# Seven half-depth products in place of eight: the last output projection of a two-layer trunk kernel, with its conditioning moved into layer 1

## The chip, the core and the metric

The kernel runs on one core of a Trainium2 chip. A core has a matrix engine (PE, with a weight-load side PEld), a vector engine (DVE), a scalar engine (ACT), a general engine (POOL) and a queue engine (SP). Each takes its instructions in order. PE writes only to PSUM, 8 banks of 512 fp32 per partition; all else lies in SBUF, 128 partitions wide. Loads are issued on SP's queue, most stores on POOL's. The metric is the device time of one execution in microseconds, as the median of several runs.

## The reference

Two transformer layers act on 640 tokens (512 latent, 128 context) of width 2048, in fp32. What is changed belongs to the end of layer 1:

```python
m = jax.nn.silu(cond) @ w + b            # modulation: shift, scale, gate of a layer
...
y_c = o_c...reshape(b, t, C_W) * jax.nn.silu(cg)
y_d = merge_heads(attend(q_d, dk_all, dv_all)) * jax.nn.silu(dg)
return jnp.concatenate([y_c, y_d], axis=-1) @ w_out, new
...
xp = xp + gt_p * out_p
xs = xs + gt_s * out_s
```

So the output projection of layer 1 is a product of a 2048 x 2048 weight with the 2048 x 640 transposed activations y, and each output row is scaled by a gate `gt` that comes from the conditioning and added to the residual.

## The kernel before

Activations are kept transposed: 128 channels on the partitions, 640 tokens along the row, so y is 16 tiles `y[k]` of 128x640. A projection is cut into output tiles of 128 channels. One tile sums over 16 channel blocks k, in four quarters of four. fp32 accuracy is had from two reduced-precision parts: `split` (L211) writes hi = ACT copy and lo = DVE subtraction, for weights (`wh`, `wl`, 128x512 for a quarter) and for activations (`h`). For each k, `proj_q` (L237) issues three matmuls (L244 to L246: wh·hi, wh·lo, wl·hi) on each half of the tokens, HV, 320 columns each, into PSUM `pa` and `pb`. A tile is thus 16 x 3 x 2 = 96 matmuls of 320 columns.

`run_tiles` (L277) runs a list of tiles. The first three ("leads") are computed together, quarter by quarter, while `make_h` brings in the activations; the third uses the PSUM of attention, `Sp`. After that tile follows tile. `run_ahead` (L322) keeps weight loads (`raw`) 5 and splits 3 quarters ahead, with 4 buffers each. After every quarter `slot` (L269) advances unfinished work: `prep` (what follows a finished tile), `attn` (attention of a head pair) and a filler at a given rate.

The filler is the conditioning, `ada_on_dve` (L171): for a block of 512 columns, 16 loads `adaw` and 32 DVE multiply-adds of 128x512 (L182, L184), then four matmuls with ones (L190) and two transposes (L196) on PE. The last three blocks (`fill2`) give the gate of layer 1 and run in the last projection (L1153), one step for each quarter.

In that last projection `y_maker` (L670) loads y back from DRAM (`yin<-yd`, L677), but for tiles 6, 7, 14 and 15, which are still in SBUF. `fin_job` (L1120) then loads the residual (`xr<-xd`), adds the gated tile to it (`fin_sum`, L1117, three DVE operations), transposes five blocks back to rows (L396), copies them (ACT, L1128 and L1129) and stores them from POOL's queue (L1130, L1131). The last tile is done in halves (`fin_last`, L1134) and stored from SP's and ACT's queues.

The order on each engine is made by a scheduler when the program is built: it may move instructions of an engine past each other where their data allow it.

## Time and profile before

| what | value |
|---|---|
| median of 3 runs | 2360.15 us (2356.45 to 2361.38) |
| the profiled execution, its own time | 2359.36 us |
| its span in the profile | 2357.6 us |
| granted clock of PE, mean | 0.996 |
| HBM read, written | 273.62 MB, 27.79 MB |
| DMA packets | 370061, 304.08 MB, mean 129 GB/s |
| first matmul of the last projection, from the span's start | 2115.3 us |

The profile is one execution. Busy time alone doesn't say what sets the end; the chain of waits (the work that ended last, followed back) and the tables by stretch do. A matmul's recorded time overlaps with that of the next one, since they are pipelined: the pace of PE is read from the distance of starts.

### The profile page before, as it was taken

What the parts mean: (1) busy time and instruction counts of PE and PEld (TensorE: products, weight loads), DVE (VectorE), ACT (ScalarE), POOL (GpSimd) and SP (SyncE); (2) the same over time, 40 slices, a digit from 0 to 9 for tenths busy, and PEclk for the clock granted to TensorE, in tenths of its full rate; (3) what the DMA queues carried; (4) which work ended last, traced back from release to release, by engine and by line L of the source; (5) the groups of instructions that cost most, each with busy time, mean ns of one, the idle gap of its engine ahead of it and who ended that gap; (6) DMA issues with size and microseconds to landing.
All of it is one profiled execution on the core that took longest, in us unless ns stands there. A gap on an engine that the chain in (4) does not pass through costs nothing.

```text
span 2357.6 us, 40891 instructions
## 1 busy us (share of the span) xinstructions
PE 2321.4 (98%) x16188; PEld 2244.9 (95%) x16188; DVE 1372.3 (58%) x2728; ACT 870.4 (37%) x1837; POOL 126.9 (5%) x173
## 2 busy tenths in 40 slices
PE   6999999999999999999999999999999999999999
PEld 3788999999999999999999999999999999999999
DVE  4458766756845565667955445354445554576662
ACT  4325442433422223222553444334334434453221
POOL 0001000000000000000010100001000000000000
PEclk8999999999999999999999999999999999999999
DMA  9984425425444445666431222212221212236552
GB/s 324 324 268 136 138 75 160 137 59 160 139 130 125 146 135 187 192 192 196 129 92 57 79 72 72 73 51 86 63 77 55 70 56 71 72 112 216 182 172 78
DMA packets 370061, 304.08 MB, mean 129 GB/s; under 512 B 16737, under 2 KB 310174, under 8 KB 369358
## 3 DMA queue, kind: packets, MB, share of 16 engines
q1 hardware_dynamic: 362464, 273.78, 38.2%
q0 software_dynamic: 6864, 27.47, 3.1%
q8 instruction: 127, 2.08, 0.3%
q14 instruction: 64, 0.52, 0.1%
q10 hardware_dynamic: 542, 0.22, 0.0%
HBM read 273.62 MB, written 27.79 MB: 128 GB/s over the span
## 4 chain that ended last, share of the span: by engine, by line
PE 93%; DMA 2%; DVE 2%; ACT 1%; issue 1%; SPq 0%; POOL 0%; ACTq 0%; DVEq 0%; POOLq 0%
PE pa L244 13%; PE pb L244 13%; PE pb L245 13%; PE pb L246 13%; PE pa L245 13%; PE pa L246 13%; PE T L545 2%; PE S L557 1%; PE S L559 1%; PE S L558 1%; PE T L158 1%; PE T L396 1%; PE T L606 1%; DMA ada<-in_ada_w 1%; PE T L608 1%
## 5 line engine op out<-in xcount | busy, mean ns | idle before, releaser
L212 ACT ACTIVATE wh<-raw 128x512 fp32r<-128x512 f32 (+1 forms) x550 | 344.0, 626 | 1044.9 <-PE pb L245 925.9
L213 DVE TENSOR_TENSOR wl<-raw,wh 128x512 fp32r<-128x512 f32 (+1 forms) x550 | 375.4, 683 | 552.5 <-ACT wh L212 501.1
L244 PE MATMUL pa<-h,wh 128*128 128x320 f32 x2112 | 669.9, 317 | 1.8 <-ACT h L747 1.2
L245 PE MATMUL pa<-h,wh 128*128 128x320 f32 x2112 | 655.8, 311 | 0.4 <-DVE h L213 0.4
L244 PE MATMUL pb<-h,wh 128*128 128x320 f32 x2112 | 654.3, 310 | 0.0
L246 PE MATMUL pa<-h,wl 128*128 128x320 f32 x2112 | 654.0, 310 | 0.0
L246 PE MATMUL pb<-h,wl 128*128 128x320 f32 x2112 | 653.9, 310 | 0.0
L245 PE MATMUL pb<-h,wh 128*128 128x320 f32 x2112 | 653.4, 309 | 0.0
L244 PEld LDWEIGHTS pa<-h,wh 128*128 128x128 f32 x2112 | 397.3, 188 | 22.0 <-issue 16.4
L245 PEld LDWEIGHTS pa<-h,wh 128*128 128x128 f32 x2112 | 398.4, 189 | 4.4 <-issue 3.3
L246 PEld LDWEIGHTS pb<-h,wl 128*128 128x128 f32 x2112 | 396.7, 188 | 2.5 <-issue 2.5
L246 PEld LDWEIGHTS pa<-h,wl 128*128 128x128 f32 x2112 | 397.3, 188 | 0.8 <-issue 0.8
L244 PEld LDWEIGHTS pb<-h,wh 128*128 128x128 f32 x2112 | 396.9, 188 | 0.5 <-ACT h L747 0.4
L245 PEld LDWEIGHTS pb<-h,wh 128*128 128x128 f32 x2112 | 396.9, 188 | 0.4 <-issue 0.4
L184 DVE SCALAR_TENSOR_TENSOR acc<-adaw,sT,acc 128x512 f32<-128x512 f32 x480 | 338.1, 744 | 18.4 <-DMA adaw<-in_ada_w 17.9
L531 ACT ACTIVATE p<-S,nm,rq 128x768 f32<-128x768 f32 (+3 forms) x120 | 101.2, 844 | 108.8 <-DVE nm L526 80.6
L524 DVE TENSOR_REDUCE nm<-S 128x1 f32<-128x768 f32 (+3 forms) x120 | 91.9, 766 | 23.3 <-PE S L559 22.6
L212 ACT ACTIVATE pth<-T 128x512 fp32r<-128x512 f32 (+1 forms) x132 | 65.8, 533 | 69.6 <-PE T L545 67.4
L213 DVE TENSOR_TENSOR ptl<-T,pth 128x512 fp32r<-128x512 f32 (+1 forms) x132 | 77.3, 608 | 5.2 <-ACT pth L212 3.9
L545 PE MATMUL T<-ident,p 128*128 128x128 f32 x452 | 64.5, 273 | 0.1
L465 ACT COPY qsw<-qx 32x512 f32<-32x512 f32 x96 | 59.3, 618 | 5.6 <-DVE m L441 4.2
L668 POOL DMA_DIRECT2D yd<-y x32 | 18.0, 562 | 750.4 <-DVE y L823 515.4
(251 smaller groups left out, 2295.2 us busy)
## 6 DMA issues: line engine op xcount, KB each, us to landing
adaw<-in_ada_w SPq DMA_DIRECT2D x256, 256.0 KB, 2.9
raw<-in_od_w_in SPq DMA_DIRECT2D x208, 256.0 KB, 2.8
raw<-in_ev_w_in SPq DMA_DIRECT2D x202, 256.0 KB, 3.0
ada<-in_ada_w SPq DMA_DIRECT2D x16, 2048.0 KB, 10.5
raw<-in_ev_w_out SPq DMA_DIRECT2D x64, 256.0 KB, 3.9
raw<-in_od_w_out SPq DMA_DIRECT2D x64, 256.0 KB, 2.7
yd<-y POOLq DMA_DIRECT2D x32, 320.0 KB, 2.9
yin<-yd SPq DMA_DIRECT2D x28, 320.0 KB, 4.6
```

The costliest lines, as they stand in the source:

```text
L158: PE.matmul(acc[32 * g:32 * g + 32, 0:wd], sT[:, kt, :], w[:, kt % m, :], start=(kt < 4), stop=(kt >= KT - 4), tile_position=(0, 32 * g))
L184: V.scalar_tensor_tensor(out=acc[c], in0=w, scalar=sT[:, kt, c:c + 1], in1=acc[c], op0=ALU.mult, op1=ALU.add)
L212: A.activation(hi, x, AF.Copy)
L213: V.tensor_sub(lo, x, hi)
L244: PE.matmul(ps, wh[:, i, :], hi[:, sl], start=(j == js[0] if alone else (pos == 0 and j == 0)), stop=False)
L245: PE.matmul(ps, wh[:, i, :], lo[:, sl], start=False, stop=False)
L246: PE.matmul(ps, wl[:, i, :], hi[:, sl], start=False, stop=(j == js[1] - 1 if alone else (pos == 3 and j == 3)))
L396: PE.transpose(t[:, i * P:(i + 1) * P], src(b), ident)
L465: A.copy(sw[32 * d:32 * d + 32, :], x[32 * (d ^ 1):32 * (d ^ 1) + 32, 0:NS])
L524: V.tensor_reduce(nm, s, axis=AX.X, op=ALU.max, negate=True)
L531: A.activation(p[:, 0:n], s, AF.Exp, scale=rsc, bias=nm, accum_out=l)
L545: PE.transpose(t[:, i * P:(i + 1) * P], p, ident)
```

## The change

Tiles 0 to 3 of the last projection are computed as before (0 to 2 as leads, 3 alone). Tiles 4 to 15 go in six pairs. A pair is a product of a 2x2 block matrix of weights (two tiles by two halves of the 16 k blocks: A11, A12, A21, A22) with a 2x2 block matrix of activations (two halves of k by two halves of the tokens: B11, B12, B21, B22). `run_pairs` does it with seven products in place of eight, Q1, Q2, N5, P6, P7, Q3, P4 in this order, each of 8 k blocks x 3 = 24 matmuls of 320 columns into a bank `pq`.

The weight sums (N5: A21+A22, P6: that plus A11, P7: A11+A21, Q3: that plus A12) are made by DVE on fp32 weights, in `sx` and `sf`, ahead of the split. The sums of activations T1 to T4 are the same for all pairs: `forms` makes them once, four DVE subtractions of 320 columns and a split of 960 for each of 8 k, from a second load of y (`yf`, 16 loads). T1 replaces the second token half of `h[0..7]` after tile 3 has used it; so tile 3 takes its second half first. The seven results are combined by DVE (`z`, `u2`, `u4` in `room`, the tables of the rotary embedding, which are free by then).

The conditioning blocks of `fill2` go into layer 1's input projection, as six half blocks of 256 columns (`ada_halves_on_dve`: loads `hadaw`, DVE steps into `hacc`, then two matmuls and two transposes), at 0.6 steps for each quarter. All 16 y tiles now pass through DRAM (`save_y` for 6 and 7 too). The SBUF pool of layer 1 ("odd") is closed after the first two quarters of the leads, and a new one ("fin") opened.

```diff
-FILL2 = 1.0
+FILL2 = 0.6
...
+    def ada_halves_on_dve(blocks):
+        for l, cb in blocks:
+            for h in range(2):
...
+                for kt in range(KT):
+                    w = ap.tile([P, 256], F32, tag="hadaw", name="hadaw", bufs=3)
+                    nc.sync.dma_start(w, I["ada_w"][l, kt * P:(kt + 1) * P, cb * 512 + h * 256:cb * 512 + (h + 1) * 256])
...
+                            V.scalar_tensor_tensor(out=acc[c], in0=w, scalar=sT[:, kt, c:c + 1], in1=acc[c],
+                                                   op0=ALU.mult, op1=ALU.add)
+                    yield
...
+    def run_pairs(cols, w_ap, mov, room, begin, done, more):
...
+        def load(p, name):
...
+            if name == "A22":
+                st8[p, name] = [load_raw(w_ap, c1, qd) for qd in (2, 3)]
+            else:
+                st8[p, name] = load8("w8", c1 if name == "A21" else c0, 8 if name == "A12" else 0, 4)
...
+            if name == "N5":
+                x = st8["x"] = ap.tile([P, W8, P], F32, tag="sx", name="sx", bufs=1)
+                for i in range(2):
+                    V.tensor_add(halves(x)[i], halves(a("A21"))[i], a("A22")[i])
+                return halves(x)
+            if name == "P6":
+                V.tensor_add(st8["x"], st8["x"], a("A11"))
+                f = st8["f"] = ap.tile([P, W8, P], F32, tag="sf", name="sf", bufs=1)
+                V.tensor_add(f, a("A11"), a("A21"))
+                return halves(st8["x"])
...
+            if name == "Q3":
+                V.tensor_add(st8["x"], st8["x"], a("A12"))
+                return halves(st8["x"])
...
+        def after(p, name, ps):
+            if name == "Q1":
+                A.copy(q1, ps)
+                begin(p)
+            elif name == "Q2":
+                V.tensor_add(z, ps, q1)
+                done(p, 0, 0, z)
+            elif name == "N5":
+                st8["n5"] = ps
+            elif name == "P6":
+                V.tensor_sub(u2, ps, q1)
+                V.tensor_sub(u4, st8["n5"], u2)
+            elif name == "P7":
+                V.tensor_sub(z, ps, u4)
+                done(p, 1, 1, z)
+                V.tensor_add(u2, ps, u2)
+                more(p, u2)
+            elif name == "Q3":
+                V.tensor_add(u4, ps, u4)
+                done(p, 0, 1, u4)
+            else:
+                done(p, 1, 0, ps)
...
+            for h in range(2):
+                wh, wl = parts[2 * i + h]
+                for j in range(4):
+                    hi, lo = rows_(4 * h + j)
+                    PE.matmul(ps, wh[:, j, :], hi, start=(h == 0 and j == 0), stop=False)
+                    PE.matmul(ps, wh[:, j, :], lo, start=False, stop=False)
+                    PE.matmul(ps, wl[:, j, :], hi, start=False, stop=(h == 1 and j == 3))
+                if h == 0:
+                    ahead(2 * i + 1)
+            after(p, name, ps)
+            ahead(2 * i + 2)
+            if name == "Q1":
+                load(p + 1, "A11")
+            elif name in ("P6", "P7"):
+                load(p + 1, "A12" if name == "P6" else "A21")
...
-            if not load:
-                save_y(i)
+            save_y(i)
...
-    run_tiles(jobs, I["od_w_in"][0], h1_maker, by_half=True)
+    run_tiles(jobs, I["od_w_in"][0], h1_maker, fill2, FILL2, by_half=True)
...
+    def y1_maker(k):
+        if k == 4:
+            for _ in fill2:
+                pass
+            drain(attn)
+            close("odd")
+            open_pool("fin")
+            attn.append(forms())
...
+    def forms():
...
+            V.tensor_sub(x3, b12, b22)
+            V.tensor_sub(x2, b11, x3)
+            V.tensor_sub(x4, b21, x2)
+            V.tensor_sub(d, b11, b12)
+            t = ap.tile([P, 2, 3 * HALF], F32R, name=f"T{j}")
+            split(t[:, 0, :], t[:, 1, :], x)
...
-    run_tiles([(n * P, fin_job(n)) for n in range(KT)], I["od_w_out"][0],
-              y_maker(("P",), 768, (6, 7, 14, 15)), fill2, FILL2, order=(0, 2, 1, 3), last=fin_last)
+    go_on = run_tiles([(n * P, fin_job(n)) for n in range(N_SINGLE - 1)], w1, y1_maker, order=(0, 2, 1, 3))
...
+    for hv in (HV[1:], HV[:1]):
+        for qd in range(4):
+            proj_q(pp, parts[qd], qd, qd, hv)
+            advance(attn, 2)
+            go_on()
+        if hv == HV[1:]:
+            drain(attn)
+            for j in range(8):
+                hi, lo = hs[j]
+                split(hi[:, HALF:NT], lo[:, HALF:NT], t1[j])
...
+    run_pairs([(n * P, (n + 1) * P) for n in range(N_SINGLE, KT, 2)], w1,
```

What the change does to the order of the engines is shown at three places. The first is SP's queue at the start of the last projection (`yin`, `yf`: y from DRAM; `raw`: weights; `adaw`: conditioning; the number behind `yd` less 128 is k). Before:

```order
L677 DMA yin<-yd_138 128x640
L1112 DMA xr<-xd_149 128x640
L677 DMA yin<-yd_139 128x640
L225 DMA raw<-in_od_w_out 128x4x128
L677 DMA yin<-yd_132 128x640
L225 DMA raw<-in_od_w_out 128x4x128
L677 DMA yin<-yd_133 128x640
L225 DMA raw<-in_od_w_out 128x4x128
```

and now, at the same k:

```order
L1272 DMA yin<-yd_139 128x640
L256 DMA raw<-in_od_w_out 128x4x128
L1272 DMA yin<-yd_132 128x640
L1272 DMA yin<-yd_133 128x640
L1272 DMA yin<-yd_134 128x640
L1283 DMA yf<-yd_128 128x640
L1283 DMA yf<-yd_136 128x640
L1272 DMA yin<-yd_135 128x640
L1283 DMA yf<-yd_129 128x640
L1283 DMA yf<-yd_137 128x640
```

The conditioning's loads are gone from this place, and 16 second loads of y stand between those of y and of the weights.

The second is DVE in the middle of the last projection. Before, an ordinary tile and the next:

```order
L1117 SCALAR_TENSOR_TENSOR xr<-pa,hgt_121,xr 128x320
L1117 SCALAR_TENSOR_TENSOR xr<-pb,hgt_121,xr 128x192
L1117 SCALAR_TENSOR_TENSOR xr<-pb,hgt_121,xr 128x128
L213 TENSOR_TENSOR wl<-raw,wh 128x512 x4
L1117 SCALAR_TENSOR_TENSOR xr<-pa,hgt_121,xr 128x320
```

and now, from Q2's result (`tables<-pq`, L491) to P6's (L496) of the second pair:

```order
L491 TENSOR_TENSOR tables<-pq,tables 128x320
L244 TENSOR_TENSOR wl<-sx,wh 128x512
L1312 SCALAR_TENSOR_TENSOR xr<-tables,hgt_121,xr 128x320
L468 TENSOR_TENSOR sx<-sx,w_24767 128x1024
L244 TENSOR_TENSOR wl<-sf,wh 128x512 x2
L463 TENSOR_TENSOR sf<-w_24936,w_25097 128x1024
L244 TENSOR_TENSOR wl<-sx,wh 128x512
L496 TENSOR_TENSOR tables<-pq,tables 128x320
```

Here w_24767 is A12 of this pair, w_24936 and w_25097 are A11 and A21 of the next one; A21 of the next pair is loaded into the buffer that A12 of this one leaves after L468. The next pair's `sf` stands ahead of Q3's split of `sx`.

The third is DVE in layer 1, in the softmax of a differential head (L671 maximum, L684 reciprocal, L1169 the weights of the second map added). Before:

```order
L526 TENSOR_SCALAR nm<-nm,rq_16639 128x1
L1042 TENSOR_SCALAR on<-T,rl 128x256
L537 RECIPROCAL rl<-l 128x1
L1022 SCALAR_TENSOR_TENSOR w<-l,nlam,rl 128x1
L1023 SCALAR_TENSOR_TENSOR p<-p,w 128x768
L1046 TENSOR_SCALAR ssq<-ssq 128x1
```

and now, with the conditioning's steps (`hacc`) among them:

```order
L673 TENSOR_SCALAR nm<-nm,rq_18482 128x1
L1188 TENSOR_SCALAR on<-T,rl 128x256
L215 TENSOR_SCALAR hacc_19127<-hadaw,sT 128x256
L684 RECIPROCAL rl<-l 128x1
L215 TENSOR_SCALAR hacc_19128<-hadaw,sT 128x256
L1168 SCALAR_TENSOR_TENSOR w<-l,nlam,rl 128x1
L217 SCALAR_TENSOR_TENSOR hacc_19127<-hadaw,sT,hacc_19127 128x256
L1169 SCALAR_TENSOR_TENSOR p<-p,w 128x768
```

The 192 steps stand in six bunches of 32, three of them in stretches without a softmax, as far as the rows go, and three beside softmaxes; some 48 steps stand between two rows of one softmax.

At the end of the program the five transposes of tile 14 now stand behind tile 15's last three on PE, and its two copies, which POOL's stores follow, behind tile 15's last copy of 384 columns on ACT. Before, tile 14 was done with before tile 15's last matmuls.

179 lines of the change are left out of this document (151 added, 28 removed).

## The prediction

> **What bounds the kernel now.** The page first: PE is busy nearly all the span, and the chain of waits, followed back from the end, lies on it almost throughout.
>
> ```profile
> PE 2321.4 (98%) x16188; PEld 2244.9 (95%) x16188; DVE 1372.3 (58%) x2728; ACT 870.4 (37%) x1837; POOL 126.9 (5%) x173
> ...
> PE 93%; DMA 2%; DVE 2%; ACT 1%; issue 1%; SPq 0%; POOL 0%; ACTq 0%; DVEq 0%; POOLq 0%
> ```
>
> Busy PE alone is not PE at its pace, so I read the table by stretch next: window, length, then busy time (and count) of PE, PEld, DVE, ACT and POOL, the clock, the DMA share and GB/s. The rows are layer 0 with the filler, layer 1's input projection, the start of the last projection (two rows) and the rest of it.
>
> ```profile
> 300.00:900.00 600.00, 599.78 (x4212) 589.93 (x4211) 372.59 (x732) 184.48 (x392) 14.70 (x19) 1.00 0.42 125
> 1230.00:2050.00 820.00, 819.10 (x5722) 804.53 (x5721) 409.94 (x853) 349.60 (x776) 54.68 (x71) 1.00 0.22 66
> 2106.00:2116.00 10.00, 9.36 (x66) 8.57 (x64) 8.81 (x20) 5.24 (x11) 1.14 (x2) 1.00 0.92 303
> 2116.00:2161.00 45.00, 45.00 (x309) 45.00 (x308) 38.28 (x60) 15.84 (x25) 0.00 (x0) 1.00 0.76 241
> 2161.00:2341.00 180.00, 179.98 (x1256) 177.59 (x1255) 88.83 (x160) 42.22 (x81) 18.27 (x29) 1.00 0.51 158
> ```
>
> The clock is full. From 2161 on PE has all the time and DVE half; at the start of the projection DVE and DMA are nearly full as well. Third, the chain in order of time gives PE's pace (start, length, what): five transposes end each tile's turn.
>
> ```profile
> 2281.68 0.55 PE T L396 x5
> ...
> 2296.31 0.55 PE T L396 x5
> ...
> 2307.42 0.57 PE T L190 x8
> ...
> 2311.93 0.55 PE T L396 x5
> ```
>
> From 2281.68 to 2296.31 is one tile: 14.63 us, less 0.55 for the transposes, by 96 matmuls is 0.1467 us for a matmul. The next turn takes 15.62 us because a conditioning block lies in it: 0.99 us of PE for a block. Last, what paces the weights:
>
> ```profile
> 2154.03 0.63 ACT L212 ACTIVATE wh<-raw 128x512 fp32r<-128x512 f32 x1 [2.89 <-PE pb L245]
> ```
>
> ACT sat idle 2.89 us until PE let go of a weight buffer: conditioning waits for PE, not PE for it. A matmul taken away in this stage is worth 0.147 us until one of the others catches up.
>
> **The change part by part.** *Matmuls.* Six pairs take 6 x 7 x 24 = 1008 matmuls of 320 columns in place of 12 x 96 = 1152; weight loads go one with each. 144 x 0.1467 = **21.1 us less**. The Trainium skill (TensorE: Matmul & The Clock Gate, "Back-to-back issue gap") gives N/2.4 + 2.5 ns at full clock, 136 ns for 320 columns; by it the saving would be an estimated 19.6 us. The trace's 147 ns decides, since the distance of tiles contains nothing else.
>
> *The conditioning on PE.* Three blocks of 0.99 us leave the last stage; six half blocks enter layer 1. A half block has half the matmuls and as many transposes, so it lies between 0.5 and 0.99 us; I take 0.68, nearer the half, since its transposes are half as wide. 6 x 0.68 - 3 x 0.99 = **+1.1 us** (0 to +3).
>
> *The conditioning on DVE.* The prices come from the groups on DVE (count, busy, mean ns, idle before):
>
> ```profile
> L184 DVE SCALAR_TENSOR_TENSOR acc<-adaw,sT,acc 128x512 f32<-128x512 f32 x90 | 62.8, 744 | 9.7 <-DMA adaw<-in_ada_w 9.7
> L213 DVE TENSOR_TENSOR wl<-raw,wh 128x512 fp32r<-128x512 f32 x62 | 42.4, 686 | 67.6 <-ACT wh L212 61.3 <-PE T L396 6.2
> L213 DVE TENSOR_TENSOR h<-yin,h 128x640 fp32r<-128x640 f32 x12 | 9.8, 820 | 1.7 <-ACT h L212 1.7
> L1117 DVE SCALAR_TENSOR_TENSOR xr<-pa,hgt,xr 128x320 f32<-128x320 f32 x15 | 8.2, 546 | 9.7 <-PE pa L246 9.6
> L1117 DVE SCALAR_TENSOR_TENSOR xr<-pb,hgt,xr 128x192 f32<-128x192 f32 x15 | 6.2, 411 | 12.8 <-PE pb L246 12.8
> L1117 DVE SCALAR_TENSOR_TENSOR xr<-pb,hgt,xr 128x128 f32<-128x128 f32 x15 | 5.1, 340 | 0.0
> ...
> L438 DVE SCALAR_TENSOR_TENSOR m<-kg,tables 128x256 f32<-128x256 f32 x8 | 3.4, 419 | 0.0
> ```
>
> 192 steps of 256 columns cost about 0.42 each (0.74 at most, as for 512): 81 us on a DVE that is busy 410 of 820 us, so 60%, no more than the 62% (372.59 of 600) of layer 0 with its filler. What it could delay is a softmax, for whose end PE's transposes wait. Layer 1 without filler, then layer 0 with it:
>
> ```profile
> L545 PEld LDWEIGHTS T<-ident,p 128*128 128x128 f32 x250 | 29.2, 141 | 1.3 <-DVE y L797 0.6
> ...
> L545 PEld LDWEIGHTS T<-ident,p 128*128 128x128 f32 x114 | 12.7, 141 | 0.7 <-DVE p L617 0.6
> ```
>
> PE idled 1.3 us before 250 transposes without filler and 0.7 us before 114 with it: per transpose the same. Half of the bunches stand where no softmax runs, with DVE's own idle time as cover; without it a step costs 0.42. Some 48 steps stand inside softmaxes, one to three in each, and what these have to spare is worked out under the third rival: 1.2 us, so two steps hide and a third may not. The 96 loads of 128 KB pass on SP's queue at 22% DMA. **+1.0 us** (0 to 5: a quarter us for each of some 20 softmaxes).
>
> *The start of the last projection.* DVE must do, from the first activation split to the first pair's weights: 16 h splits (0.82), 8 forms of four 320-column subtractions and a 960-column one (0.49 and 1.16, by the slope from 512 to 640 columns, 1.05 ns an element), 12 weight splits, the gated sums of four tiles (1.30 each), 8 splits of T1 (0.49), the last gate (1.8) and two pair splits: 13.1 + 25.0 + 8.2 + 5.2 + 3.9 + 1.8 + 1.4 = 58.6 us. Instructions overlap a little, though:
>
> ```profile
> 2148.36 3.39 DVE L184 SCALAR_TENSOR_TENSOR acc<-adaw,sT,acc 128x512 f32<-128x512 f32 x5
> ...
> 2113.62 0.82 DVE L213 TENSOR_TENSOR h<-yin,h 128x640 fp32r<-128x640 f32 x1 [0.39 <-ACT h L212]
> ...
> 2115.30 0.42 PE pa L244
> ```
>
> Five of 0.744 took 3.39, 0.08 less each; with some 90 instructions 51 us remain. PE needs 4 x 14.08 + 1.65 = 58.0 us from 2115.30, and DVE starts 1.7 us ahead: 8 us to spare. Most of it goes in waits in order: the fourth weight split of tile 3 can't start until PE frees a buffer, 42.2 us in, and the three leads' sums come at 35, 39 and 42. Walked through, DVE is done with Q1's weights at about 56 of 58.0. Loads: 32 of y, 10 weight quarters, 3 residuals and 2 MB for the first pair are 16 MB, 53 us at the 303 GB/s seen above, for which there are some 66 us. SP's queue is the risk: a second load of y waits until DVE has used the form two before it, and weights and later y are queued behind. The last link is A21 of the first pair, loaded into the buffer that the last form frees at about 55.
>
> ```profile
> xb<-in_x_sample SPq DMA_DIRECT2D x8, 512.0 KB, 5.1
> raw<-in_od_w_out SPq DMA_DIRECT2D x64, 256.0 KB, 2.7
> yin<-yd SPq DMA_DIRECT2D x28, 320.0 KB, 4.6
> out_y_sample<-ot POOLq DMA_DIRECT2D x15, 256.0 KB, 3.8
> out_y_prompt<-ot POOLq DMA_DIRECT2D x15, 64.0 KB, 3.3
> ```
>
> 512 KB lie between 2.7 and 5.1 us to landing; with 0.4 to issue it is there at 58 to 60.5. The sums for N5 stand ahead of Q2's splits, 4.5 us in all, to be done by 63.8: 0 to 1.2 us late. Each of the last four forms could come one landing late, 4 x (4.6 - 2.7) = 7.6. I take **+1.5 us** (0 to 8).
>
> *The pairs.* DVE for a pair: 14 splits 9.6, two sums of 512 1.4, three of 1024 at 1.22 3.7, six of 320 at 0.49 2.9, gated sums 3 x 0.55 + 2 x 0.75 = 3.1: 20.7 us against PE's 168 x 0.1467 + 10 x 0.11 = 25.7. The tight place is the next pair's `sf`, ahead of Q3's split. With Q2's end as zero, DVE does z, a split, a sum and L468 (0.49 + 0.69 + 0.55 + 1.22, and 0.25 until it sees Q2) and frees A12's buffer at 3.2; A21 of the next pair lands at 6.3 to 8.7; `sf` and the split end at 8.2 to 10.6; Q3 starts at 3 x 3.52 = 10.56. On time: **+0.5 us** (0 to 3).
>
> *The end.* Before:
>
> ```profile
> 2352.54 0.43 DVE xr L1117
> 2353.11 0.53 PE T L1145 x3
> 2353.66 0.38 ACT ot L1146
> ...
> 2161.66 0.59 ACT L1128 COPY ot<-T 128x512 f32<-128x512 f32 x1
> 2162.14 0.27 ACT L1129 COPY ot<-T 128x128 f32<-128x128 f32 x1
> ...
> L1130 POOL DMA_DIRECT2D out_y_sample<-ot x15 | 11.4, 759 | 208.1 <-ACT ot L1129 208.1
> L1131 POOL DMA_DIRECT2D out_y_prompt<-ot x15 | 8.1, 539 | 0.3 <-issue 0.3
> ```
>
> Now tile 14's five transposes and copies stand behind tile 15's. On the old clock: eight transposes from 2353.1 end at 2354.2; ACT copies 384 columns (some 0.48, between 0.38 and 0.59), 512 and 128 until 2355.0; POOL issues 0.76, then the prompt's store from 2356.0, 3.3 to land: 2359.3 against a span of 2357.6. **+1.7 us** (+1 to +2.5).
>
> Sum, on the profiled execution's own 2359.4 (0.8 under the median, inside the spread of the three runs): 2359.4 - 21.1 + 1.1 + 1.0 + 1.5 + 0.5 + 1.7 = 2344.1. **2344 us.**
>
> **The rivals.** *Starved start.* The loads of y and SP's order, not PE, pace the first 60 us. For it: DMA share 0.92 and DVE 88% at 2106; against: with the conditioning's loads in it PE still had 45.00 of the 45 us from 2116 at 241 GB/s. All four late forms: +7.6 instead of +1.5, 2350. If a gap gets long, the Trainium skill (the same page, "Why this matters for your kernels") wants no idle over about 3 us, or the clock falls to half; no run here shows such a gap.
>
> *Pairs paced by DVE or A21.* If A21 takes 2 us longer to land than 5.1, Q3 waits so in each of the five pairs that have a successor: +10, 2354. Against it: this stretch moves 133 GB/s (3.4 MB in 25.7 us), less than the 158 before.
>
> *Slower.* The conditioning in layer 1's softmaxes holds PE.
>
> ```profile
> 2075.92 0.62 DVE L617 TENSOR_SCALAR p<-p,rl 128x768 f32<-128x768 f32 x1
> ...
> 2077.74 0.87 PE T L545 x8
> ```
>
> The weights of a softmax are ready at 2076.54 and PE wants them at 2077.74: 1.2 us to spare. To turn the sign, each of the 96 pairs of steps (0.84 us) would have to hold PE for over 15.3 / 96 = 0.16 us: the late softmaxes would have to set back their successors, so that the pairs beside them count too. At 0.25 us each it is 24 us, 2367. For it: three bunches stand beside softmaxes; against it: DVE is 50% busy here, the other half of the steps has no softmax near, and layer 0 shows nothing of it. That the seven products don't save PE time can't be: the count of matmuls is in the program.
>
> **How the numbers follow.** Forecast 0.70, starved start 0.13, paced pairs 0.08, slower 0.09. All stalls at zero and the half blocks at 0.5 give 2359.4 - 21.1 + 1.0 = 2339; one under it for the spread of runs: 2338. Upward the range takes in the first two rivals: 2354. A measurement here can tell 0.2%, 4.7 us: faster is under 2355.4, which the first two cases and most of the third give; slower over 0.2% is the fourth and a little of all. Faster 0.85, same 0.05, slower 0.10.
>
> **What would show it.** Right: transposes of a pair's tiles 25.7 us apart from pair to pair, PE's idle before `pq` matmuls under 3 us in all, `wh` in the pairs still waiting for PE, layer 1's input projection as long as before within 2 us, the last stage (from its first matmul) 222 us in place of 242. Wrong: idle on PE ended by DMA `yf`, `w8` or by DVE `h`, `T`, `sx`; by DVE L617 in layer 1; a stretch with the clock under 1.00.

## The result and the profile after

The changed kernel takes 2356.50 us (median of 20 runs, 2350.83 to 2361.65) where the kernel before takes 2359.61 (20 runs, 2356.22 to 2362.06): ratio 0.9986 [0.9979, 0.9993]. That is 3.1 us or 0.14% faster: the interval leaves out 1, but the gain is under the 0.2% up to which the prediction speaks of the same time. Forecast were 15.3 us less, 2344, and a range of 2338 to 2354.

The page of the changed kernel, first its line of busy times, then the shares of the chain that ended last:

```profile
PE 2309.2 (98%) x16050; PEld 2229.7 (95%) x16050; DVE 1477.3 (63%) x2982; ACT 905.9 (38%) x1898; POOL 130.3 (6%) x175
...
PE 79%; issue 12%; DVE 3%; DMA 2%; ACT 1%; POOL 1%; SPq 1%; ACTq 0%; POOLq 0%; DVEq 0%
```

PE's busy time fell by 12 us and the span by 2.7 only. The 12% "issue" are no waits of PE: the chain now ends in POOL's stores of tile 14 and runs back along POOL's queue, store behind store, while PE works. In order of time, beside the second pair (start, length, what):

```profile
2223.95 0.75 POOL out_y_sample L1320
2224.70 0.61 issue
2225.33 0.53 POOL out_y_prompt L1321
2225.86 19.47 issue
```

So I read stages, in the table of stretches (window, length, then busy time and count of PE, PEld, DVE, ACT and POOL, clock, DMA share, GB/s). Each is bounded by the starts of two matmuls of the projections that are the same ones in both kernels. Before, in order: the first keys of layer 1 (from the 193rd to the 385th matmul of its input projection), the rest of that projection up to its last tile, the last projection up to its last matmul, and from there to the end of the span:

```profile
1183.77:1215.53 31.76, 30.56 (x212) 29.45 (x210) 16.24 (x31) 16.10 (x41) 1.77 (x2) 1.00 0.38 112
1215.53:2078.36 862.83, 861.36 (x6014) 845.01 (x6012) 433.08 (x898) 371.94 (x829) 61.62 (x78) 1.00 0.23 68
2114.50:2352.20 237.70, 237.19 (x1645) 234.53 (x1643) 128.91 (x223) 59.93 (x110) 19.51 (x31) 1.00 0.54 170
2352.20:2357.59 5.39, 0.82 (x6) 0.38 (x4) 0.96 (x3) 0.37 (x1) 0.00 (x0) 0.81 0.13 37
```

The same for the changed kernel; its last projection is cut at the first matmul of the first pair, of the second and of the third (the rows of the later pairs, 25.72 each as well, are left out):

```profile
1183.93:1218.97 35.04, 31.90 (x213) 31.01 (x211) 27.43 (x61) 16.32 (x40) 1.86 (x2) 0.95 0.56 165
1218.97:2090.68 871.71, 868.40 (x6051) 847.39 (x6048) 493.07 (x1072) 373.86 (x835) 63.88 (x78) 1.00 0.27 79
2126.64:2187.66 61.02, 58.61 (x402) 57.88 (x400) 50.72 (x90) 31.20 (x52) 4.41 (x7) 1.00 0.94 301
2187.66:2218.57 30.91, 27.70 (x181) 27.15 (x179) 22.44 (x37) 10.13 (x18) 1.29 (x2) 0.94 0.44 122
2218.57:2244.29 25.72, 25.72 (x182) 25.70 (x180) 19.41 (x33) 10.53 (x20) 2.58 (x4) 1.00 0.46 133
2346.86:2354.85 7.99, 1.62 (x11) 0.94 (x9) 0.55 (x1) 1.19 (x3) 1.29 (x2) 0.90 0.23 67
```

Up to the first keys the two stand alike (1183.77 and 1183.93), partly by luck, as the next paragraph says. Then the changed kernel loses 3.3 us at the first keys and 8.9 in the rest of layer 1, gains 17.5 in the last projection (220.2 for 237.7) and loses 2.6 at the end; the last tile of layer 1 gives 0.2 back. The sum is -2.7, the difference of the spans. Two of these rows have a clock under 1.00 in mid-kernel: the first keys and the first pair.

A stretch that no row shows moves by itself from profile to profile: the first 192 matmuls of layer 1's input projection, which end before the first conditioning step. There the clock falls to 0.50 for 6.83 us in some profiles (the changed kernel from 1151.81 to 1158.64, and e2, e8, e10, e11, e12, e16 below), for 3.41 us in others (the kernel before from 1154.03 to 1157.44, and e7), and not at all in the rest; the stretch takes 34.9 to 35.4, 33.9 to 34.1 and 32.6 us. Differences of one profile's span, or of the whole input projection, hold up to 2.8 us of this, whatever the kernel.

**The first keys.** The chain in order of time, changed kernel (start, length, what):

```profile
1202.51 2.29 DMA hadaw<-in_ada_w
...
1204.89 0.49 DVE hacc L217 x2
...
1206.48 0.69 DVE kg L570
...
1211.59 0.40 DVE hacc L217
1211.98 0.61 DVE m L588
1212.59 0.04 issue
1212.64 0.66 PE T L543 x4
1213.30 0.20 PE pa L275
1213.49 0.27 PE pa L276
```

The key's first product `kg` stands on DVE behind conditioning steps, and these wait for their own load. The last sum of its rotation, `m`, stands behind one more step. PE needs `m` for four transposes and waits. The summed waits of PE in layer 1 (waited for: us, times, longest), before and then changed:

```profile
PE T L396 <- DVE m L441: 0.8, 2, 0.4
```

```profile
PE T L543 <- DVE m L588: 4.3, 3, 3.1
```

Behind the wait, matmuls come every 0.267 us, which the stretches around it show as the clock:

```profile
1209.00:1213.00 4.00, 0.86 (x7) 0.62 (x7) 4.00 (x9) 1.29 (x3) 0.60 (x1) 1.00 0.30 84
1213.00:1217.00 4.00, 4.00 (x20) 3.96 (x19) 3.19 (x7) 2.96 (x6) 0.00 (x0) 0.57 0.56 163
```

So the wait of 3.1 us costs more behind it: ten matmuls at half clock, 10 x 0.12 = 1.2 us.

**The start of the last projection and the first pair.** The timeline of DVE around Q1 and Q2 (start, length, what, idle before and its releaser):

```profile
2184.74 1.29 DVE L244 TENSOR_TENSOR wl<-w,wh 128x512 fp32r<-128x512 f32 x2 [0.19 <-ACT wh L243]
2189.07 1.29 DVE L458 TENSOR_TENSOR sx<-w,raw 128x512 f32<-128x512 f32 x2 [3.04 <-DMA w<-in_od_w_out]
2190.28 0.68 DVE L244 TENSOR_TENSOR wl<-w,wh 128x512 fp32r<-128x512 f32 x1
```

and of PE:

```profile
2187.81 0.31 PE L519 MATMUL pq<-h,wh 128*128 128x320 f32 x1
2191.02 0.42 PE L520 MATMUL pq<-h,wl 128*128 128x320 f32 x1 [2.90 <-DVE wl L244]
```

Q1's two splits are done at 2186.0. DVE then waits 3.04 us for A21, for the two sums of N5 that stand ahead of Q2's split (2190.28). PE wants that split at 2187.96, ahead of all of Q1: the program's order on PE has nine matmuls of Q2 (`h8` to `h10`, split `wl_24602` of A12) in front of Q1's first:

```order
L277 MATMUL pa_24422<-h15_24258,wl_24390 128x320
L518 MATMUL pq_24660<-h8_23978,wh_24601 128x320
L519 MATMUL pq_24660<-h8_23978,wh_24601 128x320
L520 MATMUL pq_24660<-h8_23978,wl_24602 128x320
```

SP's queue shows when A21's load was issued; it is the first of the three that begin at 2181.94, behind a residual that waited 3.90 us:

```profile
2177.64 3.90 SPq L1307 DMA_DIRECT2D xr<-xd  x1
2181.94 10.56 SPq L434 DMA_DIRECT2D w<-in_od_w_out  x3
```

Twelve matmuls at half clock follow PE's wait. Some 15 us earlier PE waits 2.3 us at the transposes of lead 1, for ACT's copy of lead 0's rows to free PSUM. ACT's timeline:

```profile
2172.15 1.00 ACT L243 ACTIVATE T<-tx 128x960 fp32r<-128x960 f32 x1 [3.24 <-DVE tx L1297]
2173.06 0.61 ACT L243 ACTIVATE wh<-raw 128x512 fp32r<-128x512 f32 x1
2173.58 0.56 ACT L1318 COPY ot<-T 128x512 f32<-128x512 f32 x1
```

The copy stands behind a split of a form that DVE has not made yet. Transfers are near full here. The stretch of 70 us from the first load of y on, before and then changed:

```profile
2108.00:2178.00 70.00, 69.36 (x477) 68.54 (x476) 51.10 (x84) 26.21 (x46) 5.01 (x8) 1.00 0.72 234
```

```profile
2120.00:2190.00 70.00, 65.64 (x447) 64.16 (x445) 56.62 (x102) 35.88 (x60) 5.48 (x9) 1.00 0.91 289
```

70 us at 289 GB/s are 20.2 MB.

### The profile page after: what moved, and what is told of

Its sections match the earlier page's. It is cut to its first block, busy times and chain, and to the rows that moved or that the text cites. A ratio compares the mean times of both kernels' runs of the same rounds, so it can differ in the third digit from the quotient of the medians.

```text
span 2354.9 us, 41103 instructions
## 1 busy us (share of the span) xinstructions
PE 2309.2 (98%) x16050; PEld 2229.7 (95%) x16050; DVE 1477.3 (63%) x2982; ACT 905.9 (38%) x1898; POOL 130.3 (6%) x175
## 4 chain that ended last, share of the span: by engine, by line
PE 79%; issue 12%; DVE 3%; DMA 2%; ACT 1%; POOL 1%; SPq 1%; ACTq 0%; POOLq 0%; DVEq 0%
PE pa L275 11%; PE pb L276 11%; PE pb L275 11%; PE pb L277 11%; PE pa L276 11%; PE pa L277 11%; PE T L692 2%; PE S L706 1%; PE S L705 1%; PE S L704 1%; PE T L158 1%; DMA ada<-in_ada_w 1%; PE T L753 1%; PE T L755 1%; PE T L754 1%
## 5 line engine op out<-in xcount | busy, mean ns | idle before, releaser
L275 PE MATMUL pa<-h,wh 128*128 128x320 f32 x1920 | 610.4, 318 | 1.5 <-ACT h L894 1.2
L276 PE MATMUL pa<-h,wh 128*128 128x320 f32 x1920 | 597.9, 312 | 0.6 <-DVE h L244 0.6
L277 PE MATMUL pa<-h,wl 128*128 128x320 f32 x1920 | 596.1, 310 | 0.0
L275 PE MATMUL pb<-h,wh 128*128 128x320 f32 x1920 | 595.1, 310 | 0.0
L277 PE MATMUL pb<-h,wl 128*128 128x320 f32 x1920 | 594.5, 310 | 0.0
L276 PE MATMUL pb<-h,wh 128*128 128x320 f32 x1920 | 594.3, 310 | 0.0
L275 PEld LDWEIGHTS pa<-h,wh 128*128 128x128 f32 x1920 | 361.9, 189 | 22.0 <-issue 16.9
L276 PEld LDWEIGHTS pa<-h,wh 128*128 128x128 f32 x1920 | 362.9, 189 | 5.0 <-issue 3.3
L277 PEld LDWEIGHTS pb<-h,wl 128*128 128x128 f32 x1920 | 360.8, 188 | 2.5 <-issue 2.5
L276 PEld LDWEIGHTS pb<-h,wh 128*128 128x128 f32 x1920 | 360.9, 188 | 0.8 <-issue 0.8
L275 PEld LDWEIGHTS pb<-h,wh 128*128 128x128 f32 x1920 | 360.9, 188 | 0.6 <-ACT h L894 0.4
L184 DVE SCALAR_TENSOR_TENSOR acc<-adaw,sT,acc 128x512 f32<-128x512 f32 x390 | 275.5, 745 | 10.2 <-DMA adaw<-in_ada_w 9.8
L671 DVE TENSOR_REDUCE nm<-S 128x1 f32<-128x768 f32 (+3 forms) x120 | 91.9, 766 | 18.4 <-PE S L706 17.8
L217 DVE SCALAR_TENSOR_TENSOR hacc<-hadaw,sT,hacc 128x256 f32<-128x256 f32 x180 | 78.0, 478 | 3.1 <-DMA hadaw<-in_ada_w 2.9
L520 PE MATMUL pq<-h,wl 128*128 128x320 f32 x192 | 60.1, 313 | 2.9 <-DVE wl L244 2.9
```

The costliest lines, as they stand in the source:

```text
L184: V.scalar_tensor_tensor(out=acc[c], in0=w, scalar=sT[:, kt, c:c + 1], in1=acc[c], op0=ALU.mult, op1=ALU.add)
L217: V.scalar_tensor_tensor(out=acc[c], in0=w, scalar=sT[:, kt, c:c + 1], in1=acc[c], op0=ALU.mult, op1=ALU.add)
L275: PE.matmul(ps, wh[:, i, :], hi[:, sl], start=(j == js[0] if alone else (pos == 0 and j == 0)), stop=False)
L276: PE.matmul(ps, wh[:, i, :], lo[:, sl], start=False, stop=False)
L277: PE.matmul(ps, wl[:, i, :], hi[:, sl], start=False, stop=(j == js[1] - 1 if alone else (pos == 3 and j == 3)))
L520: PE.matmul(ps, wl[:, j, :], hi, start=False, stop=(h == 1 and j == 3))
```

## The experiments

All times of the stages below are read as above. "Keys" is the stretch of the first keys, "rest" that up to layer 1's last tile, "start" from the first matmul of the last projection to the second pair's first, "end" from the sixth pair's first matmul to the end of the span. The ratio is to the kernel before, with its 95% interval.

| kernel | median us | ratio | keys | rest | start | end |
|---|---|---|---|---|---|---|
| before | 2359.6 | 1 | 31.8 | 862.8 | | |
| changed | 2356.5 | 0.9986 [0.9979, 0.9993] | 35.0 | 871.7 | 91.9 | 33.4 |
| e1_few_steps | 2348.7 | 0.9959 [0.9947, 0.9971] | 31.8 | 869.5 | 91.3 | 33.4 |
| e2_joined | 2352.2 | 0.9974 [0.9964, 0.9984] | 35.2 | 868.8 | 91.7 | 33.6 |
| e3_gated | 2353.6 | 0.9979 [0.9970, 0.9988] | 31.8 | 872.8 | 95.0 | 33.4 |
| e4_no_reload | 2349.2 | 0.9959 [0.9945, 0.9972] | 36.1 | 871.7 | 87.5 | 33.4 |
| e5_joined_gated_tail | 2346.4 | 0.9947 [0.9935, 0.9960] | 31.8 | 867.2 | 91.9 | 31.4 |
| e6_p4_third | 2354.9 | 0.9986 [0.9977, 0.9995] | 33.5 | 871.8 | 91.2 | 33.4 |
| e7_pool_p4 | 2350.2 | 0.9969 [0.9957, 0.9981] | 34.4 | 872.1 | 88.0 | 33.1 |
| e8_half_reload | 2353.1 | 0.9972 [0.9960, 0.9984] | 34.7 | 871.7 | 89.8 | 33.4 |
| e9_four | 2341.4 | 0.9929 [0.9916, 0.9941] | 31.8 | 867.5 | 88.5 | 31.5 |
| e10_four_own | 2345.0 | 0.9942 [0.9929, 0.9955] | 31.8 | 867.3 | 92.7 | 31.5 |
| e11_all6 | 2344.3 | 0.9943 [0.9931, 0.9955] | 31.8 | 867.3 | 92.4 | 31.6 |
| e12_half_forms | 2351.2 | 0.9965 [0.9954, 0.9976] | 35.1 | 871.8 | 85.8 | 33.4 |
| e13_banks | 2351.3 | 0.9964 [0.9952, 0.9977] | 35.3 | 871.8 | 88.9 | 33.4 |
| e14_best_banks | 2340.5 | 0.9923 [0.9910, 0.9936] | 31.8 | 867.2 | 87.6 | 31.4 |
| e15_poolform | 2342.3 | 0.9928 [0.9915, 0.9942] | 31.8 | 867.5 | 89.3 | 31.5 |
| e16_four_banks | 2342.6 | 0.9926 [0.9913, 0.9939] | 31.8 | 867.5 | 86.8 | 31.4 |

"Start" moves by itself: of the five kernels that leave that stage alone, four lie at 91.3 to 92.0 (changed, e1, e2, e5) and one at 95.0 (e3). So does "keys", from 33.5 to 36.1 in the eight kernels that leave the steps where they are (e2 only joins them); "rest" stays within 0.5 us (871.7 to 872.1) where nothing in it is changed. The stages are those of one profiled execution, the median is of several.

**e1: the steps, almost all left out.**

```diff
                 for kt in range(KT):
+                    if kt > 0:
+                        yield
+                        continue
                     w = ap.tile([P, 256], F32, tag="hadaw", name="hadaw", bufs=3)
```

> Leaves out, in layer 1, fifteen of the sixteen loads and pairs of DVE steps of each half block (so the gate values of the last layer are wrong); the half blocks' matmuls and transposes on PE stay. Theory (the steps queue on DVE ahead of the first key's rope, PE waits there over 3 us and its clock falls): the wait before the first key's transposes falls from 3.1 us to about 0.4, no matmul there is at 0.267 us, and layer 1's input projection, 978.1 us in the changed kernel, takes 972 to 974; the kernel about 2351. Rival one (the softmaxes pay, the key's chain is slow by itself): the wait before the key stays above 2 us, gain 1 to 2 us. Rival two (layer 1 grew by the blocks' PE time alone): gain under 1 us.

Keys 31.75 as before the change, longest wait for `m` 0.4 us, no matmul there at 0.267 us: the theory's first half holds. The rest falls by 2.2 us as well, so the steps cost 3.3 + 2.2 = 5.5 us in all, and the median fell more than expected (2348.7 for 2351). The input projection's 969.7 us, for 972 to 974 expected, is no better than the theory: 2.8 us of its gain lie ahead of the first step, in the stretch that moves by itself. 869.5 stays 6.7 us above the 862.8 before: the half blocks on PE.

**e2: one group of matmuls for both halves.**

```diff
-                    PE.matmul(s[32 * c:32 * c + 32, 0:256], ones, acc[c], start=True, stop=True,
-                              tile_position=(0, 32 * c))
+                if h == 0:
+                    continue
+                for g in range(4):
+                    PE.matmul(s[32 * g:32 * g + 32, 0:256], ones, both[g], start=True, stop=True,
+                              tile_position=(0, 32 * g))
```

> The two halves of a block keep their DVE steps, but share one group of four ones matmuls and one pair of transposes. Theory (the ones matmuls of different column groups run beside each other, so a half block, 1.21 us of PE, costs more than half of a whole one, 0.99): three groups of about 0.99 in place of six of 1.21, 4.3 us less PE time; against it the first bunch has now 64 steps without a break beside the first keys, so that wait may grow by 0 to 3 us; the kernel 2352 to 2355, and the six places where the halves' matmuls stood show 0 or 0.99. Rival (cost by the count of matmuls, 0.68 a half as predicted): 1.1 us less, 2355.4 or more.

Timeline of PE, the group of a half block in the changed kernel and that of a whole block in e2 (the count is two records for a matmul):

```profile
1330.77 0.63 PE L222 MATMUL T<-hacc,ones 128*32 128x256 f32 x4
```

```profile
1685.62 0.64 PE L225 MATMUL T<-hacc,ones 128*32 128x256 f32 x8
```

Twice the matmuls in the same time. The transposes behind them, of 64 rows in the changed kernel and of 128 rows in e2, with a matmul of the projection before and after:

```profile
1331.87 0.31 PE L277 MATMUL pb<-h,wl 128*128 128x320 f32 x1
1332.11 0.33 PE L228 MATMUL T<-ident,hsb 64*128 64x64 f32 x2
...
1332.63 0.31 PE L276 MATMUL pb<-h,wh 128*128 128x320 f32 x1
```

```profile
1686.74 0.31 PE L279 MATMUL pa<-h,wh 128*128 128x320 f32 x1
1686.88 0.38 PE L231 MATMUL T<-ident,hsb 128*128 128x128 f32 x2
...
1687.25 0.31 PE L281 MATMUL pa<-h,wl 128*128 128x320 f32 x1
```

From the first start to the last are 0.76 and 0.51 us, less two matmuls at 0.147. So, counted between the starts of the projection's matmuls around them, a half block takes 0.75 + 0.46 = 1.21 us and a joined one 0.76 + 0.22 = 0.98: 4.3 us less on PE, as expected. What lifts a half block above a whole one is its two transposes: 0.46 us in all six half blocks, 0.22 in all three joined ones. The stage gained 2.9 only; that bunches of 64 steps cost more beside them is a guess that no run shows. The count of matmuls as the price of a block is refuted.

**e3: no step before the second key's rope.**

```diff
+            V.scalar_tensor_tensor(out=sTb, in0=m1[:, 0, 0:2 * KT].rearrange("p (k c) -> p k c", c=2), scalar=0.0,
+                                   in1=sT[:, :, 0:2], op0=ALU.mult, op1=ALU.add)
...
+        while "sTb" not in st:
+            yield
+        sT = st["sTb"]
```

> The conditioning's steps read a copy of the scaled condition that is made from the second key's rope, so none of them can run before it; the rate is 0.68 in place of 0.6, all else as in the changed kernel. Theory (the first bunch in the first key's way): the wait of 3.1 us before the first key's transposes and the half clock behind it go, layer 1's input projection 978.1 to about 974.4, the kernel about 2352.8. Rival (the steps then stand in the way of the next queries, keys or softmaxes, and the same time is lost there): input projection 977 or more.

Keys 31.75: the whole loss there is gone. The rest grew by 1.1 us, so 2.2 us of the 3.7 expected are left: the theory holds, less two fifths of its gain. The input projection's 973.0 us look better than the 974.4 expected, but 2.8 us of that lie ahead of the first keys, in the stretch that moves by itself.

**e4: second loads of y left out.**

```diff
-            (ya, yb), nxt = nxt, (load(j + 1) if j < 7 else None)
+            ya, yb = nxt
```

> Leaves out 14 of the 16 second loads of y: all eight forms are made from the first pair of y tiles (so the sums of activations are wrong); DVE's and ACT's work is the same. Theory (transfers pace the start of the last projection: 20 MB at 300 GB/s in 69 us): the wait of 2.4 us before the third lead's transposes falls under 0.5, the 3.07 us in the first pair and the half clock behind it go; first matmul of the last projection to first pair 61.0 to about 58, first pair 30.9 to about 26; the kernel 2348 to 2350. Rival (DVE's own work paces it): under 2 us less.

Start 87.5 for 91.9: 4.4 us of the 7 expected, and below all five starts that nothing touches. PE still waits 1.7 us for `wl` and 1.5 for ACT's copy. Transfers are over half of it, not all. The median, 2349.2, lies in the 2348 to 2350 expected, 7.3 us under the changed kernel's; the two intervals allow 4.4 as well.

**e5: joined, held back, and tile 14's rows inside the last product.**

```diff
                 if h == 0:
                     ahead(2 * i + 1)
+                    if i == len(seq) - 1:
+                        slot()
```

> Halves joined on PE and steps held back until the second key's rope, as in the two runs before, and at the end tile 14's rows are made in the middle of the last product instead of behind it. Theory: the stretch of the first keys 31.75 us as without steps (35.0 in the changed kernel), the rest of layer 1's input projection to its last tile 868 to 869 (871.7), from the last product's last matmul to the end of the span 6.2 in place of 8.0; together 7 to 8 us less, 2349. Rival for the joining (64 steps in a bunch cost elsewhere what PE gains): the rest of the projection 871 or more. Rival for the end (POOL's stores set it anyway, or tile 14's transposes hold up the last product): no gain or under 0.5 us.

Keys 31.8, rest 867.2, end 31.4 for 33.4: all three gains are there, both rivals fall. In the rest they are 2.7 us more than the two runs before add up to (871.7 - 2.9 + 1.1 = 869.9); why is not shown.

**e6 and e7: P4 third in the first pair; then its sums with A21 on POOL too.**

```diff
+        first = ("Q1", "Q2", "P4", "N5", "P6", "P7", "Q3")
+        seq = [(p, n) for p in range(len(cols)) for n in (first if p == 0 else MOV)]
...
-                    V.tensor_add(halves(x)[i], halves(a("A21"))[i], a("A22")[i])
+                    (G if p == 0 else V).tensor_tensor(halves(x)[i], halves(a("A21"))[i], a("A22")[i], op=ALU.add)
...
-                V.tensor_add(f, a("A11"), a("A21"))
+                (G if p == 0 else V).tensor_tensor(f, a("A11"), a("A21"), op=ALU.add)
```

> In the first pair P4, which needs no A21, is made third, ahead of N5. Theory (the sums that need A21 stand on DVE ahead of Q2's split, so DVE, not N5's matmuls, waits for the load): moving the product changes little, the first pair takes 28 to 31 us (30.9 in the changed kernel; 27.6 to 31.4 in the runs so far) and PE still waits for Q2's wl by 1.5 to 3 us. Rival (N5 itself is what A21 holds up): first pair 26.5 or less.

> As the run before, and the first pair's two sums with A21 (for N5 and P7) are made on POOL instead of DVE, so DVE's queue never waits for A21. Theory (the in-order wait on DVE): no wait for Q2's wl, first pair 26 to 27 us; the kernel 2352. Rival (DVE is simply late with its own work, or the load with A12): the wait for wl stays above 1.5 us. Rival (POOL is too slow for 1024 columns): a wait of PE ended by POOL sx or sf in the first pair, over 1 us.

e6: a wait of 1.4 us for `wl`, first pair 27.9, both a shade under what was expected; as in kernels that change nothing there (28.0, 28.3, 28.5 in e1, e2, e5). e7: no wait for `wl`, none for POOL, first pair 25.8. So what waited was DVE's queue, in order.

**e8: half the second loads.** Tiles 4 to 7 and 12 to 15 of y stay in SBUF until their forms are made, ahead of the others:

```diff
+            if j >= 4:
+                ya, yb = held[j], held[j + 8]
+            else:
+                (ya, yb), nxt = nxt or load(j), (load(j + 1) if j < 3 else None)
```

> Complete kernel with 8 second loads of y in place of 16: the tiles 4 to 7 and 12 to 15 of y are kept from their first load until their forms are made, which come first. Theory (transfers pace the start; 14 loads less gave 4.4 us): from the last projection's first matmul to the second pair's first 91.9 us becomes 88.5 to 90, the kernel 2353 to 2355. Rival (buffers held longer hold up the loads that come after): no gain, or a loss up to 3 us.

Start 89.8, 2.1 us less than the changed kernel and 1.5 less than the lowest start that nothing touches; the wait for ACT's copy 1.4 us, that for `wl` still 2.6.

**e9: the four mends that hold** (e5's and e7's, no new edit).

> The mends so far together, complete kernel: halves joined, steps held back until the second key, tile 14's rows inside the last product, first pair with P4 third and its two A21 sums on POOL. Theory (the parts are additive, each in its own stage): first keys 31.75, rest of layer 1's input projection 867.2, first matmul of the last projection to the second pair's first 88 us (91.9), end 31.4 us from the sixth pair's last product but one (33.4); 12 us under the changed kernel, 2343 to 2345. Rival (the pieces meet in the last projection, the gain of one is lost in another wait): 2347 or more.

They add: 2341.4. The wait for ACT's copy is left, 2.6 us.

**e10 and e11: other PSUM for the leads' rows; then half the loads too.**

```diff
+        ta, tb = new_pp(n) if n in (1, 2) else (None, None)
-        A.copy(ot[:, 0:4, :], to_rows(cols_of(xr), True).rearrange("p (b f) -> p b f", b=4))
+        A.copy(ot[:, 0:4, :], to_rows(cols_of(xr), True, ta).rearrange("p (b f) -> p b f", b=4))
```

> As the run before, and the rows of leads 1 and 2 are transposed into their own PSUM banks, so PE need not wait for ACT to copy the rows of the lead before. Theory (ACT, in order, stands in a split of forms that waits for DVE, and behind it the copies that free PSUM): the wait of 2.1 to 2.6 us for ACT ot and the half clock behind it go, first matmul to second pair 85 to 86.5; 2341 to 2343. Rival (DVE's gated sums are as late as ACT's copies): PE waits at the same transposes for DVE xr, under 1 us gained.

> As the run before, and with 8 second loads of y in place of 16. Theory (transfers, the load of A21 and the order on DVE and ACT are all that delays the start): first matmul of the last projection to second pair 84 to 85, the least it can take without a wait being about 84.3 (384 x 0.1467, three sets of transposes at 0.57 and 25.7 to 25.8 for a pair); 2340 to 2342. Rival (with waits gone the load order no longer matters): same as the run before within 1 us.

Both miss: start 92.7 and 92.4. PE now waits 2.9 and 4.3 us for ACT's copies at the third lead's own bank. The wait only moved.

**e12: four of the eight forms left out.**

```diff
-        for j in range(8):
+        for j in range(4):
...
+        T.extend(T[:4])
+        t1.extend(t1[:4])
```

> The changed kernel with forms for four of the eight k alone, used twice (so the sums of activations are wrong): 8 second loads of y are left out, as in the run with half the reloads, and besides them half of the forms' subtractions and splits on DVE and ACT. It tells what is left of the wait for ACT's copies of the leads' rows, 2.3 us in the changed kernel and 1.4 to 1.5 with 8 or 14 loads less. Theory (ACT, in order, stands in a split of a form that DVE has not reached, so it is the forms' work): that wait under 0.3 us, first matmul of the last projection to first pair 58.4 to 59. Rival (transfers alone): the wait 1.4 us as with the loads alone, 59.7.

The wait for ACT's copy is gone, and that for `wl`: first pair 25.8. So DVE's and ACT's work on the forms takes part, not the loads alone. First matmul to first pair stays 59.95, though, as in e8: PE waits 0.8 us for DVE's gated sums there, and the 58.4 to 59 were not reached.

**e13: the pairs' banks rotated.** Q1 of the first pair was put in the bank that tile 3 fills last; Q2's bank is free sooner, which is why nine of its matmuls went ahead.

```diff
-tag=f"p{'ab'[i % 2]}{i // 2 % 2}", name="pq")
+tag=f"p{'ab'[i % 2]}{(i // 2 + 1) % 2}", name="pq")
```

> The seven products take the four banks in another rotation, so Q1 of the first pair gets a bank that is free and not the one that tile 3 fills; PE then has Q1's 24 matmuls ahead of Q2's. DVE's order (sums with A21 ahead of Q2's split) is as in the changed kernel. Theory (the bank lets Q2 go ahead of Q1, and so PE wants Q2's split 3.5 us sooner than it need): Q1 hides the load, the wait for wl falls from 2.9 us to under 0.6, no half clock there, first pair 25.8 to 26.5; 5 us less, 2351 to 2352. Rival (A21 is later than that, DVE's order alone decides): the wait for wl stays above 1.5 us, first pair 27.6 or more.

PE has Q1 first, the wait for `wl` is gone, and no half clock follows; DVE's order is as it was. First pair 27.3, between the 25.8 to 26.5 of the theory and the 27.6 of the rival, because tile 3's transposes now wait 1.4 us for DVE. That is 3.6 us under the changed kernel's profile, but only 0.7 under e1's: the order and the wait are shown, the size lies between 0.7 and 4 us. The median is 2351.3, as expected.

**e14 to e16: the mends of layer 1 and of the end with the banks; the forms' upper parts on POOL as well; the banks with e9's mends.**

```diff
-            split(t[:, 0, :], t[:, 1, :], x)
+            G.tensor_copy(t[:, 0, :], x)
+            V.tensor_sub(t[:, 1, :], x, t[:, 0, :])
```

> Complete kernel: halves joined, steps held back until the second key, tile 14's rows inside the last product, and the banks rotated; no sums on POOL and the products in the old order. Theory: as the four mends before, with the rotation in the place of POOL's sums; first matmul of the last projection to second pair 88 to 89, 2341 to 2343. Rival (bank alone leaves part of the wait): 2344 or more.

> As the run before, and the upper parts of the forms are rounded on POOL instead of ACT. Theory (ACT, in order, holds the copies of lead 0's rows behind a split of a form): the wait of PE for ACT ot falls from 2.1 to 2.6 us to under 0.5, first matmul to first pair 59 to 60 in place of 61 to 63.6; 2338 to 2340. Rival (POOL needs over 2 us for 960 columns, or slows DVE beside it): forms late on POOL, and the wait moves to DVE T or the sums, no gain.

> The four mends before (P4 third, POOL's sums) with the banks rotated as well. Theory (either of the two takes the whole wait away, so they don't add): as the better of the two within 0.5 us in the first pair, 25.8; 2341. Rival (each took a part): first pair below 25.7 cannot be, so a gain would have to show ahead of it.

e14 is the fastest by its median, 2340.5, though the intervals don't tell it from e9. Its stretches in the order of those above (keys, rest, first matmul to first pair, first pair, last matmul to end):

```profile
1180.65:1212.42 31.77, 30.58 (x213) 29.46 (x211) 16.18 (x31) 16.13 (x41) 1.77 (x2) 1.00 0.43 124
1212.42:2079.63 867.21, 864.53 (x6045) 846.20 (x6042) 504.83 (x1100) 373.54 (x832) 63.18 (x78) 1.00 0.28 82
2115.69:2177.63 61.94, 59.86 (x400) 59.51 (x400) 50.95 (x91) 31.06 (x52) 4.42 (x7) 0.97 0.95 302
2177.63:2203.27 25.64, 25.64 (x180) 25.63 (x179) 22.14 (x37) 10.24 (x18) 1.29 (x2) 1.00 0.45 132
2332.14:2337.61 5.47, 0.83 (x6) 0.35 (x4) 0.55 (x1) 0.48 (x1) 1.14 (x2) 0.97 0.34 97
```

The first pair runs like every other one. e15 takes the wait for ACT away (first matmul to first pair 60.5), but PE then waits 2.7 us for DVE's gated sums and 1.6 for `wl`: a cast of 960 columns takes POOL 1.35 us in the median, up to 1.99, and DVE waits for it. e16 gains nothing over e9 or e14 that the intervals tell apart, as forecast.

## Why the prediction was wrong

**Right.** The saving: a pair takes 25.72 us for two tiles of 14.63, 6 x 3.54 = 21.2 us (21.1 forecast). Pairs two to six: no wait (+0.5 forecast, the rival of paced pairs did not come). A21's load: forecast to be issued "at about 55" of the stage, it was the one at 2181.94, 55.3 after the first matmul. The direction: faster, though by the prediction's own mark (faster is under 2355.4) it is "same", which had a chance of 0.05.

**The conditioning on PE, mis-sized: +1.1, to +3 at most, was forecast; 6 x 1.21 - 3 x 0.99 = +4.3 it was** (by e1 6.7 - 3.0 = +3.7). The step that failed is "A half block has half the matmuls and as many transposes, so it lies between 0.5 and 0.99 us". Half the ones matmuls cost as much as all: those of a whole block run four beside each other, those of a half two beside each other, in the same time (e2). The Trainium skill (TensorE: Matmul & The Clock Gate, "Part 3: Packing small matmuls — row/col tiling") says that matmuls on different 32x32 tiles of the array run concurrently, some 4 ns apart; the trace agrees that they run concurrently, some 7 ns apart (0.63 us for 4 records, 0.64 for 8). And the transposes, taken as cheaper "since its transposes are half as wide", cost twice as much, 0.46 us for 0.22. The first alone would have put a half block at the upper bound; the second puts it above.

**The conditioning on DVE, +1.0 forecast, 5.5 it was, above the top of 0 to 5.** The step that failed: "Half of the bunches stand where no softmax runs, with DVE's own idle time as cover". I looked for softmaxes alone (and the two rows of transposes by which I compared the layers are of PEld, PE's weight-load side). The first bunch stands in the first key's chain, in which DVE, POOL and DVE again follow each other, and what is idle on DVE there is waiting for that chain. It cost 3.3 us (e1, e3), the half clock among it. The other bunches, softmaxes included, cost 2.2, inside the 0 to 5; in which waits, no run tells.

**The start, +1.5 forecast.** From the stages: -17.5 = -21.2 (matmuls) - 3.0 (blocks gone) - 0.55 (tile 14's transposes gone to the end) + 7.2. (The stage is counted from its first matmul, at 2114.50 before; the prediction's 2115.30 is the second, behind a wait of 0.49 us.) Two steps failed. "The sums for N5 stand ahead of Q2's splits, 4.5 us in all, to be done by 63.8: 0 to 1.2 us late" took Q1's 3.5 us as cover, without a look at PE's order, in which Q2 goes first; e13 shows it. And "16 MB, 53 us at the 303 GB/s seen above, for which there are some 66 us": 20.2 moved. The stores of y and of the leads' rows (2 MB), the next residuals and weights were left out; at 289 GB/s the 4.2 MB are 14.5 us, all of the 13 that I had to spare. So A21 let DVE go on 7.1 us after its issue (5.1 and 0.4 to issue forecast at most), and the forms came late on DVE and ACT (e4, e8, e12). In size this is rival one, the starved start, nearly at its full 7.6; in kind only in part, for leaving out the second loads gives 4.4 of it back.

**The half clock.** I put it at nothing, since "no run here shows such a gap". The two waits above each have it behind them, ten and twelve matmuls, some 1.2 + 1.4 us, which are in the terms above. And the trace before the change did show such things: a pause of 5.5 us from 27.92 us on, with half clock behind it, and half clock from 1154.03 to 1157.44 us with no pause over 1.0 us ahead of it.

**The signs named.** PE waits 3.2 us before `pq` matmuls (under 3 for right), all of it in the first pair. Layer 1's input projection takes 978.1 us for 964.6 (within 2 for right; 1.5 of the difference lie in the stretch that moves by itself). The last stage takes 228.2 us for 243.1 (222 for right). And two stretches show a clock under 1.00, a sign of being wrong.

**The end, +1.7 forecast**: 2.6 - 0.55 = +2.05, inside its bounds; e5 takes 2.0 of it away.

Together -21.2 + 3.7 + 5.5 + 7.2 + 2.05 = -2.75, the -2.7 between the spans. No single step decides: of three terms two came out above their upper ends and one near it. The range took in one rival at a time and never added two, though the terms lie in different stages and had no reason to exclude each other; added, the upper ends give 2359.4 - 21.1 + 3 + 5 + 8 + 3 + 2.5 = 2359.8.

What stays open: why the wait for `wl` in the first pair of kernels that leave it alone is now 1.5 to 2.0 us (e1, e2, e5; first pair at 28), now 2.7 to 2.9 with half clock behind it (e3, changed; at 31), and whether the last wait, for ACT's copies, can be had without another in its place; e10, e11 and e15 only moved it.

## What to carry to other kernels

Work hung on an idle engine is not free where that engine's idle time is itself a wait inside a chain; look for every in-order chain beside it, not for one kind. When a transition is costed, count all bytes of the window, stores included, and read what the consumer takes first from its own order. And add the upper ends of terms that lie in different stages before the range is drawn.
